# Transposing cached memory keys between query column tiles in a hybrid decoder layer

## The chip, the core and the metric

The kernel runs on one core of one Trainium2 chip. Its time is the device time of one execution in microseconds (us); less is better. TensorE (PE) multiplies and transposes into PSUM; VectorE (DVE), ScalarE (ACT) and GpSimd (POOL) do the rest; SyncE (SP) issues the transfers between DRAM and SBUF.

## What is computed

One inference step of one decoder layer serves two groups with the same weights: a prompt of 512 rows, and eight sampled sequences of four rows each (32 rows). Each sub-layer normalises its input and its output and adds the output to the residual. Everything is float32.

1. A mixer of two head groups (mLSTM and differential attention) with a common input and output projection.
2. Cross-attention, 4 heads of 256, into 256 memory tokens. This is the part that is changed:

```python
def mem_attend(h, mk, mv, w_mq, w_mo):
    q = (h @ w_mq).reshape(B, T, MEM_HEADS, MEM_HEAD_DIM)
    s = jnp.einsum('bqhd,bkhd->bhqk', q, mk) * (MEM_HEAD_DIM ** -0.5)
    p = jax.nn.softmax(s, axis=-1)
    o = jnp.einsum('bhqk,bkhd->bqhd', p, mv).reshape(B, T, D_MODEL)
    return o @ w_mo
```

   The prompt's memory keys and values are projected in the kernel. Those of the eight sequences come from a cache in DRAM (cache_mem_k and cache_mem_v, each 8 x 256 tokens x 1024 columns).
3. A gated feed-forward network with a causal convolution of width 3.

The outputs are both groups' rows, the new keys and values, and the new states.

## The kernel before

All work is written out in Python and recorded instruction by instruction. A scheduler then orders each engine's instructions by a simulated timeline, so the order on an engine is fixed when the program is built, and it need not be that of the source. Tiles come from pools with a fixed number of buffers, in rotation; who takes a buffer waits for the last reader of the tile before it.

**Weights.** A weight tile is loaded into one of six staging buffers (`stage`, tile name wst), and ScalarE and VectorE split it into a high and a low part (`split`, lines 142 and 143) in one of four weight slots (pool `wp`, tag W). The large matmuls multiply high by high, high by low and low by high.

**Queries.** `gemmB` (line 452) makes the query in eight column tiles of 128 columns, 48 matmuls each, over all 544 rows in two halves (256 and 288 rows, alternating). The first four tiles run by halves; the last four, m = 4 to 7, one after the other, each from its own slot. `ev_q` scales a finished tile into qh and ql (prompt) and qs (samples).

**Prompt attention.** `prompt` is a pipeline over 8 steps (head and half of the rows): `ch_soft` makes scores sca (12 matmuls) and the probabilities cp, `ch_turn` transposes them (cpt, 4 transposes) into pT, `ch_out` multiplies by the values (cpo, 12 matmuls for a head). Each `next(prompt)` gives one step of it.

**Sample attention.** Half a sequence's keys, 128 tokens x 1024, is one turn; there are 16. `mk_load` brings it into a staging buffer; `mk_turn` makes eight transposes (tpk, in two PSUM groups of four from a pool of three buffers) and copies them to kT, the first group by ScalarE, the second by VectorE (line 1385). A kT holds a sequence's keys and lies in a weight slot. `mk_scores` makes a sequence's scores: 8 matmuls ssc of 32 columns each, four of which lie beside each other in the array; then the maximum (VectorE) and the exponential (ScalarE). TensorE takes two passes for each of these float32 matmuls, so the trace counts 16 of them where the program has 8. After the eighth sequence `sample_softmax` combines the sums (spa, spt, caz). `mv_load` brings a sequence's values (vt) into a weight slot, and `mv_out` makes 8 matmuls pso with them. The output projection w_mo follows in the same slots.

What sets the order around the change is the loop over `pipe(2 * NB, mk_load, mk_turn, mk_scores)`: it starts behind the last column tile, with prompt steps at `KSTEPS` (3, 7, 11, 15) and the first two value loads at `VLOADS` (13, 15).

Of the kernel before, what the change touches and what calls it, by code (L numbers as in the profile page):

```python
# [18 lines left out]
NB = 8  # L19
# [54 lines left out]
def kernel(ctx: ExitStack, tc: tile.TileContext, I, O):  # L74
# [9 lines left out]
    KSTEPS, VLOADS, NMID, VSTEPS = (3, 7, 11, 15), (13, 15), 3, (0, 1, 3, 5, 6, 7)  # L84
# [13 lines left out]
    def S(shape, dt, name):  # L98
        return sp.tile(list(shape), dt, name=name, tag="S")
# [4 lines left out]
    def T2(shape, name, dt=F32):  # L104
        return t2p.tile(list(shape), dt, name=name, tag="T2")
# [4 lines left out]
    def at(name="at"):  # L110
        return psa.tile([P, 512], F32, name=name, tag="at")

    def mmp(name="mm"):
        return psm.tile([P, 512], F32, name=name, tag="mm")

    def small(w, name, p=P):
        return sm.tile([p, w], F32, name=name, tag=name)
# [5 lines left out]
    def v2(t, b):  # L123
        return t.rearrange("p (a b) -> p a b", b=b)
# [12 lines left out]
    def f32(ap):  # L137
        return ap.bitcast(F32)
# [12 lines left out]
    def con(n, p=P):  # L151
        o, w = CONST_COLS[n]
        return cpk[:p, o:o + w]
# [51 lines left out]
    def stage():  # L205
        return stg.tile([P, 1024], F32, name="wst", tag="st")
# [144 lines left out]
    def pipe(n, *stages):  # L351

        for t in range(n + len(stages) - 1):
            for s in reversed(range(len(stages))):
                if 0 <= t - s < n:
                    stages[s](t - s)
            yield
# [73 lines left out]
    def gemmB(xt, evacs, half_first=False):  # L431

        if half_first:
            slots = [W.get() for _ in evacs]
            for i, (c0, c1) in enumerate(HALF):
                for s, ev in zip(slots, evacs):
                    ps = mmp()[:, :c1 - c0]
                    for k in range(8):
                        for j, (l, x) in enumerate(((0, xt.hi), (0, xt.lo), (1, xt.hi))):
                            mm(ps, lhsT=s[:, l, k, :], rhs=x(k, c0, c1), start=(k == 0 and j == 0), stop=(k == 7 and j == 2))  # L440
                    if i == 1:
                        W.free()
                    ev(i, c0, c1, ps)
                    yield 2.6
            return
        for ev in evacs:
            s = W.get()
            ps = [mmp()[:, :c1 - c0] for c0, c1 in HALF]
            for k in range(8):
                for j, (l, x) in enumerate(((0, xt.hi), (0, xt.lo), (1, xt.hi))):  # L450
                    for i, (c0, c1) in enumerate(HALF):
                        mm(ps[i], lhsT=s[:, l, k, :], rhs=x(k, c0, c1), start=(k == 0 and j == 0), stop=(k == 7 and j == 2))  # L452
                if k % 2 == 1 and k < 7:
                    yield 1.36
            W.free()
            for i, (c0, c1) in enumerate(HALF):
                ev(i, c0, c1, ps[i])
            yield 1.36
# [91 lines left out]
    for i, _ in enumerate(mem_k()):  # L550
        if i in HSTEPS:
            j = HSTEPS.index(i)
# [76 lines left out]
    for c0, c1 in HALF:  # L629
# [5 lines left out]
        t = T2([64, n], "gt")  # L635
# [374 lines left out]
    def sample_exp(sall, b, ps, nm, su):  # L1010
        VRED(out=nm[:, b:b + 1], in_=ps, axis=AX.X, op=MAX, negate=True)
        ACT(out=sall[:, b, :], in_=ps, func=AF.Exp, bias=nm[:, b:b + 1], accum_out=su[:, b:b + 1])
# [294 lines left out]
    def ev_q(m):  # L1307
        if m % 2 == 0:
            qh.append(npool.tile([P, 2, 516], F32R, name="qh", tag="N"))
        if m % 4 == 0:  # L1310
            ql.append(S([P, 4, SEQ], F32R, "ql"))

        def ev(i, c0, c1, ps):
            n = min(c1, SEQ) - c0
            q = qh[m // 2][:, m % 2, c0:c0 + n]
            nc.scalar.mul(out=q, in_=ps[:, :n], mul=1.0 / 16.0)
            STT(out=ql[m // 4][:, m % 4, c0:c0 + n], in0=ps[:, :n], scalar=1.0 / 16.0, in1=f32(q), op0=MUL, op1=SUB)
            if i == 1:
                nc.scalar.mul(out=qs[:, m, :], in_=ps[:, n:n + NS], mul=1.0 / 16.0)
        return ev  # L1320
# [51 lines left out]
    def mk_load(i):  # L1372
        b, c = i // 2, i % 2
        kst[i] = stage()
        dma(out=kst[i], in_=I["cache_mem_k"][0, b, c * P:(c + 1) * P].rearrange("t h d -> t (h d)"))

    def mk_turn(i):
        b, c = i // 2, i % 2
        if c == 0:
            kts[b] = wp.tile([P, 8, 256], F32, name="kT", tag="W")  # L1380
        for q in range(2):
            ps = at("tpk")
            for j in range(4):
                tr(ps[:, j * P:(j + 1) * P], kst[i][:, (4 * q + j) * P:(4 * q + j + 1) * P], ident)  # L1384
            (VCP if q else nc.scalar.copy)(out=kts[b][:, 4 * q:4 * q + 4, c * P:(c + 1) * P], in_=v2(ps, P))

    def mk_scores(i):
        b, c = i // 2, i % 2
        if c == 0:
            return  # L1390
        ps = mmp("ssc")[:, :256]
        for c in range(2):
            for h in range(H):
                mm(ps[NS * h:NS * h + NS], lhsT=qs[:, 2 * h + c], rhs=kts[b][:, 2 * h + c, :], start=(c == 0), stop=(c == 1))  # L1394
        sample_exp(sall, b, ps, nm, su)

    def mv_load(b):
        vts[b] = wp.tile([P, 2, DM], F32, name="vt", tag="W")
        dma(out=vts[b], in_=I["cache_mem_v"][0, b].rearrange("(c p) h d -> p c (h d)", p=P))
# [7 lines left out]
    sall = S([P, NB, 256], F32, "cas")  # L1407
    nm, su = small(NB, "snm"), small(NB, "ssu")
    prompt = pipe(8, ch_soft, lambda i: None, ch_turn, ch_out)
    for i, _ in enumerate(gemmB(hqT, [ev_q(m) for m in range(4, 8)])):  # L1410
        pass
    for t, _ in enumerate(pipe(2 * NB, mk_load, mk_turn, mk_scores)):
        if t in KSTEPS:
            next(prompt, None)
        if t in VLOADS:
            mv_load(VLOADS.index(t))
    _, az = sample_softmax(sall, su, None, con("selX"), "ca")
    for _ in range(NMID):
        next(prompt, None)
# [2 lines left out]
        slotsA(w_mo, n0)  # L1422
    W.nslots = NSLOT
    for b in range(NB):
        if b >= len(VLOADS):
            mv_load(b)
    W.pump()
    for b in range(NB):
# [85 lines left out]
    class Up:  # L1514
# [5 lines left out]
        def ev(self, i, c0, c1, ps):  # L1520
            ti = self.ti
            spread(i)
            if i == 0:
                u = self.u = T2([P, EXT], "u")
                nc.gpsimd.memset(u[:, 0:2], 0.0)
                self.sv = u[:, 2 + SEQ:].rearrange("p (b j) -> p b j", j=6)
                nc.gpsimd.tensor_copy(out=self.sv[:, :, 0:2], in_=v2(cvT[:, ti, 0:16], 2))
                VTT(out=u[:, 2:258], in0=ps, in1=rsb[:, 0:256], op=MUL)  # L1528
                return
            u, sv = self.u, self.sv  # L1530
            VTT(out=u[:, 258:514], in0=ps[:, :256], in1=rsb[:, 256:SEQ], op=MUL)  # L1531
            VTT(out=sv[:, :, 2:6], in0=v2(ps[:, 256:288], TS), in1=v2(rsb[:, SEQ:], TS), op=MUL)
            nc.gpsimd.tensor_copy(out=self.cvo[:, 0:2], in_=u[:, SEQ:SEQ + 2])  # L1533
            nc.gpsimd.tensor_copy(out=v2(self.cvo[:, 2:18], 2), in_=sv[:, :, 4:6])
            c = self.c = T2([P, EXT - 2], "c")
            w = [cvT[:, ti, 16 + j:17 + j] for j in range(3)]
            VTS(out=c, in0=u[:, 2:EXT], scalar1=w[2], scalar2=cvT[:, ti, 19:20], op0=MUL, op1=ADD)
            STT(out=c, in0=u[:, 1:EXT - 1], scalar=w[1], in1=c, op0=MUL, op1=ADD)  # L1538
            STT(out=c, in0=u[:, 0:EXT - 2], scalar=w[0], in1=c, op0=MUL, op1=ADD)  # L1539
# [243 lines left out]
```

## Time and profile before

| | |
|---|---|
| median of 3 runs | 1005.29 us (1005.04 to 1005.99) |
| the profiled execution | 1005.6 us |
| its span | 1003.8 us |
| TensorE busy | 975.0 us, 97% of the span |
| granted TensorE clock, mean | 0.986 |
| last four query column tiles | from about 436 to 460 us |
| transposes and scores of cached keys | 460 to 499 us |
| value sums of the samples | 509 to 532 us |

The profile shows one execution. Times are microseconds from the start of the span, unless marked ns. A row of the order in time has the start, the length from the first instruction's start to the last one's end, engine, line, operation, output and inputs, and count; in brackets stand the idle time ahead and the instruction that ended it. TensorE's matmuls overlap: the next one starts before the last one ends.

### The profile page before, as it was taken

The page shows a single profiled execution, that of the slowest core. Times are in us where ns is not written, and L with a number is a line of the kernel's source. Part 1 is how long each engine was busy: PE and PEld are TensorE (multiplying, and loading weights), DVE is VectorE, ACT ScalarE, POOL GpSimd, SP SyncE. Part 2 cuts the span into 40 slices and gives each one's busy share as a digit, 9 for nine tenths or more (in the row PEclk, how much of TensorE's full clock was granted, in tenths as well). Part 3 has the DMA queues.
Part 4 walks back from the last instruction along what each step waited for, and adds up shares of the span by engine and source line. Part 5 has one row for each costly group of instructions (what it writes and reads, how often), then busy time and mean ns, then how long its engine had stood idle before and what let it go on. Part 6 is the DMA issues. An engine that isn't in the chain of part 4 may idle for free.

```text
span 1003.8 us, 17048 instructions
## 1 busy us (share of the span) xinstructions
PE 975.0 (97%) x6615; PEld 813.2 (81%) x6615; DVE 601.9 (60%) x1129; ACT 388.4 (39%) x746; POOL 195.4 (19%) x389
## 2 busy tenths in 40 slices
PE   8999999999799999999999999999999999999994
PEld 5899777889555778998757789979987997997983
DVE  5735324643686357634653587836857685675677
ACT  5654313334376348633442444242222222222232
POOL 6510000112332124400000264301101010110115
PEclk9999999999799999999999999999999999999998
DMA  8950224152534167764851673052142314214113
GB/s 276 302 156 20 65 84 129 43 182 60 175 115 145 40 210 255 252 206 157 325 199 42 194 236 106 26 146 86 45 116 75 96 46 126 87 44 135 34 47 110
DMA packets 120401, 130.26 MB, mean 130 GB/s; under 512 B 8423, under 2 KB 85832, under 8 KB 120320
## 3 DMA queue, kind: packets, MB, share of 16 engines
q1 hardware_dynamic: 114136, 125.69, 40.6%
q10 hardware_dynamic: 6184, 3.48, 1.2%
q8 instruction: 52, 0.85, 0.3%
q14 instruction: 29, 0.24, 0.1%
HBM read 112.22 MB, written 16.93 MB: 129 GB/s over the span
## 4 chain that ended last, share of the span: by engine, by line
PE 87%; DVE 5%; DMA 4%; issue 2%; ACT 2%; POOL 1%; ACTq 0%; SPq 0%; DVEq 0%; POOLq 0%
PE mm L452 30%; PE mm L440 7%; PE mm L386 6%; PE mm L388 6%; PE mm L387 6%; PE mm L1626 4%; PE mm L1628 4%; PE mm L1627 4%; PE mm L366 3%; PE sda L1179 2%; PE tpk L1384 1%; PE sca L1335 1%; PE cpo L1365 1%; PE ssc L1394 1%; PE oda L1205 1%
## 5 line engine op out<-in xcount | busy, mean ns | idle before, releaser
L142 ACT CAST wslot<-wst 128x1024 fp32r<-128x1024 f32 (+1 forms) x127 | 131.1, 1036 | 278.8 <-issue 81.2
L452 PE MATMUL mm<-fT,wslot 128*128 128x256 f32 (+1 forms) x1872 | 235.7, 288 | 0.0
L452 PEld LDWEIGHTS mm<-fT,wslot 128*128 128x128 f32 x1872 | 234.7, 188 | 0.7 <-issue 0.4
L143 DVE TENSOR_TENSOR wslot<-wst,wslot 128x1024 fp32r<-128x1024 f32 (+1 forms) x127 | 154.0, 1215 | 109.7 <-ACT wslot L142 109.7
L1626 PE MATMUL mm<-wslot,act 128*128 128x512 f32 (+1 forms) x176 | 70.7, 409 | 0.0
L1627 PE MATMUL mm<-wslot,act 128*128 128x512 f32 (+1 forms) x176 | 69.5, 395 | 0.0
L1628 PE MATMUL mm<-wslot,act 128*128 128x512 f32 (+1 forms) x176 | 69.0, 397 | 0.0
L1533 POOL COPY cvo<-u 128x2 f32<-128x2 f32 x43 | 16.1, 375 | 222.8 <-DVE u L1531 222.8
L386 PE MATMUL mm<-wslot,hT 128*128 128x512 f32 x128 | 51.9, 408 | 0.0
L452 PE MATMUL mm<-hT,wslot 128*128 128x288 f32 (+1 forms) x384 | 51.4, 290 | 0.0
L387 PE MATMUL mm<-wslot,hT 128*128 128x512 f32 x128 | 51.2, 400 | 0.0
L388 PE MATMUL mm<-wslot,hT 128*128 128x512 f32 x128 | 50.7, 397 | 0.0
L452 PEld LDWEIGHTS mm<-hT,wslot 128*128 128x128 f32 x384 | 48.9, 188 | 0.9 <-issue 0.8
L1626 PEld LDWEIGHTS mm<-wslot,act 128*128 128x128 f32 (+1 forms) x176 | 33.1, 189 | 17.7 <-issue 8.6
L1528 DVE TENSOR_TENSOR u<-mm,rsb 128x256 f32<-128x256 f32 x43 | 18.1, 423 | 44.2 <-PE mm L452 43.3
L1628 PEld LDWEIGHTS mm<-wslot,act 128*128 128x128 f32 (+1 forms) x176 | 33.0, 188 | 7.5
L1627 PEld LDWEIGHTS mm<-wslot,act 128*128 128x128 f32 (+1 forms) x176 | 33.1, 188 | 6.5
L1545 ACT ACTIVATE c<-c 128x560 f32<-128x560 f32 x21 | 14.1, 672 | 57.3 <-DVE c L1539 57.2
L1539 DVE SCALAR_TENSOR_TENSOR c<-u,cvT,c 128x560 f32<-128x560 f32 x43 | 34.3, 798 | 0.8
L1538 DVE SCALAR_TENSOR_TENSOR c<-u,cvT,c 128x560 f32<-128x560 f32 x43 | 34.1, 794 | 0.1
L1639 DVE TENSOR_TENSOR yp<-mm,yp 128x512 f32<-128x512 f32 x40 | 27.3, 689 | 9.5 <-PE mm L1628 9.4
L386 PEld LDWEIGHTS mm<-wslot,hT 128*128 128x128 f32 x128 | 24.0, 188 | 10.3 <-issue 5.8
(458 smaller groups left out, 1885.8 us busy)
## 6 DMA issues: line engine op xcount, KB each, us to landing
wst<-in_w_up_dram SPq DMA_DIRECT2D x42, 512.0 KB
wst<-in_w_in_dram SPq DMA_DIRECT2D x28, 512.0 KB
wst<-in_w_down_dram SPq DMA_DIRECT2D x20, 512.0 KB
wst<-in_cache_mem_k_dram SPq DMA_DIRECT2D x16, 512.0 KB
vt<-in_cache_mem_v_dram SPq DMA_DIRECT2D x8, 1024.0 KB
wst<-in_w_mk_dram SPq DMA_DIRECT2D x8, 512.0 KB
xb<-in_x_prompt_dram SPq DMA_DIRECT2D x8, 512.0 KB
wst<-in_cache_dk_dram SPq DMA_DIRECT2D x16, 256.0 KB
```

The source lines that it names most:

```text
L142: nc.scalar.copy(out=hi, in_=src)
L143: (eng or nc.vector).tensor_tensor(out=lo, in0=src, in1=f32(hi), op=SUB)
L386: mm(ps[b], lhsT=xt.hi(k, c0, c0 + n), rhs=s[:, 0, kk, :], start=(k == 0), stop=False)
L387: mm(ps[b], lhsT=xt.hi(k, c0, c0 + n), rhs=s[:, 1, kk, :], start=False, stop=False)
L388: mm(ps[b], lhsT=xt.lo(k, c0, c0 + n), rhs=s[:, 0, kk, :], start=False, stop=(k == nk - 1))
L440: mm(ps, lhsT=s[:, l, k, :], rhs=x(k, c0, c1), start=(k == 0 and j == 0), stop=(k == 7 and j == 2))
L452: mm(ps[i], lhsT=s[:, l, k, :], rhs=x(k, c0, c1), start=(k == 0 and j == 0), stop=(k == 7 and j == 2))
L1538: STT(out=c, in0=u[:, 1:EXT - 1], scalar=w[1], in1=c, op0=MUL, op1=ADD)
L1539: STT(out=c, in0=u[:, 0:EXT - 2], scalar=w[0], in1=c, op0=MUL, op1=ADD)
L1626: mm(ps, lhsT=t[:, 0, c0:c0 + P], rhs=s[:n, 0, i % 2, :], start=st, stop=False)
L1627: mm(ps, lhsT=t[:, 0, c0:c0 + P], rhs=s[:n, 1, i % 2, :], start=False, stop=False)
L1628: mm(ps, lhsT=t[:, 1, c0:c0 + P], rhs=s[:n, 0, i % 2, :], start=False, stop=en)
```

## The change

The loop over `pipe` is written out. Six key loads are issued ahead of the last four column tiles. Behind each of these tiles (every fourth step of `gemmB`) stand two turns, one sequence's keys, and the loads of the turns six later; the kT takes the slot that the column tile leaves. Then comes a loop over the sequences: its scores; for the first four, the two turns of the sequence four later; for the last four, a value load. Every second sequence a prompt step follows. So four value loads are issued in this loop instead of two.

```diff
+    for i in range(6):
+        mk_load(i)
     for i, _ in enumerate(gemmB(hqT, [ev_q(m) for m in range(4, 8)])):
-        pass
-    for t, _ in enumerate(pipe(2 * NB, mk_load, mk_turn, mk_scores)):
-        if t in KSTEPS:
+        if i % 4 == 3:
+            for j in (i // 2 - 1, i // 2):
+                mk_turn(j)
+                mk_load(j + 6)
+    for b in range(NB):
+        mk_scores(2 * b + 1)
+        if b < 4:
+            for j in (2 * b + 8, 2 * b + 9):
+                mk_turn(j)
+                if j + 6 < 2 * NB:
+                    mk_load(j + 6)
+        else:
+            mv_load(b - 4)
+        if b % 2 == 1:
             next(prompt, None)
-        if t in VLOADS:
-            mv_load(VLOADS.index(t))
...
-        if b >= len(VLOADS):
+        if b >= 4:
             mv_load(b)
```

What this makes of TensorE's order is seen at three places. The first is the border between the column tiles m = 4 and m = 5 (mm of line 452; hqT is the normalised input, wslot the weight), as a difference:

```order
 L452 MATMUL mm<-hqT_4081,wslot 128x256
 L452 MATMUL mm<-hqT_4081,wslot 128x288
+L1384 MATMUL tpk<-cpk,wst 128x128 x12
 L452 MATMUL mm<-hqT_4069,wslot 128x256
 L452 MATMUL mm<-hqT_4069,wslot 128x288
```

Twelve transposes now stand here, and the last four of the two turns 18 matmuls later, inside the next tile. The same pair of 12 and 4 stands behind m = 5 and m = 6.

The second place is among the transposes and scores (ssc) that follow the columns. Before, TensorE has there:

```order
L1394 MATMUL ssc<-kT,qs 32x256 x6
L1384 MATMUL tpk<-cpk,wst 128x128 x16
L1394 MATMUL ssc<-kT,qs 32x256 x8
L1384 MATMUL tpk<-cpk,wst 128x128 x12
L1394 MATMUL ssc<-kT,qs 32x256 x2
L1384 MATMUL tpk<-cpk,wst 128x128 x4
```

And now, directly behind the last column tile:

```order
L1384 MATMUL tpk<-cpk,wst 128x128 x12
L1394 MATMUL ssc<-kT,qs 32x256 x14
L1384 MATMUL tpk<-cpk,wst 128x128 x4
L1394 MATMUL ssc<-kT,qs 32x256 x2
L1384 MATMUL tpk<-cpk,wst 128x128 x8
```

No run of transposes is longer than 12, and scores of two sequences stand in one run of 14. The runs of scores are now 14, 2, 5, 3, 8, 8, 2, 6, 2, 6, 2, 6; before they were 2, 6, 8, 2, 6, 8, 2, 6, 2, 6, 2, 6, 2, 6. The runs of value sums (pso) are now 12, 9, 4, 1, 3, 3, 16, 8, 8; before 6, 10, 6, 4, 2, 3, 2, 15, 8, 8.

The third place is the end of the sample softmax (spa and spt) and the prompt's fifth transposes (cpt). Before:

```order
L1365 MATMUL cpo<-pT,mvN 128x512 x8
L1031 MATMUL spa<-cas,csz 32x256 x8
L1365 MATMUL cpo<-pT,mvN 128x512 x4
L1036 MATMUL spt<-cpk,spc 128x128 x2
L1353 MATMUL cpt<-cpk,cp 128x128
```

Now spa stands ahead of a whole step of prompt scores, of which this is the beginning:

```order
L1335 MATMUL sca<-mkT,ql 128x256
L1353 MATMUL cpt<-cpk,cp 128x128 x4
L1031 MATMUL spa<-cas,csz 32x256 x8
L1335 MATMUL sca<-mkT,qh 128x256 x2
L1335 MATMUL sca<-mkT,ql 128x256
```

And behind these twelve sca follow the same products and the fifth transposes:

```order
L1335 MATMUL sca<-mkT,ql 128x256
L1365 MATMUL cpo<-pT,mvN 128x512 x8
L1036 MATMUL spt<-cpk,spc 128x128 x2
L1365 MATMUL cpo<-pT,mvN 128x512 x4
L1353 MATMUL cpt<-cpk,cp 128x128
```

So 12 sca and 12 cpo lie between spa and the fifth cpt, where 4 cpo lay before. On SP, ten key loads are issued ahead of the small loads for the convolution (cr), where six were; and four loads of w_mo ahead of the first value load, where two were.

## The prediction

> **What bounds the kernel now.** I read the page first, then a table of stretches around the edit, then TensorE's instructions in order of time in those stretches.
>
> ```profile
> span 1003.8 us, 17048 instructions
> PE 975.0 (97%) x6615; PEld 813.2 (81%) x6615; DVE 601.9 (60%) x1129; ACT 388.4 (39%) x746; POOL 195.4 (19%) x389
> PE 87%; DVE 5%; DMA 4%; issue 2%; ACT 2%; POOL 1%; ACTq 0%; SPq 0%; DVEq 0%; POOLq 0%
> ```
>
> TensorE is busy for 97% of the span, and 87% of the chain that ended last is TensorE. The table (stretch, its length, then busy time of each engine, granted clock, DMA share, GB/s) holds the four last query columns, the keys and scores, the value sums, and the memory output projection.
>
> ```profile
> 436.00:460.20 24.20, 24.20 (x197) 24.20 (x196) 3.83 (x8) 4.33 (x14) 1.81 (x1) 1.00 0.24 83
> 460.20:504.40 44.20, 43.22 (x369) 31.78 (x371) 27.10 (x57) 21.00 (x61) 0.00 (x0) 1.00 0.83 291
> 504.40:534.00 29.60, 28.85 (x236) 18.02 (x235) 15.36 (x32) 14.91 (x44) 0.00 (x0) 1.00 0.40 144
> 534.00:560.00 26.00, 26.00 (x162) 18.84 (x161) 12.11 (x26) 9.71 (x21) 0.00 (x0) 1.00 0.26 76
> ```
>
> TensorE is full in all four at clock 1.00. So the columns have no idle time into which the transposes could go: the change can only pay by making TensorE's steps shorter or by removing its waits. The rows of TensorE (start, time from the first start to the last end, line, operation, count; in brackets the idle time ahead, and who ended it):
>
> ```profile
> 436.13 24.11 PE L452 MATMUL mm<-hqT,wslot 128*128 128x256 f32 x192
> 460.08 2.55 PE L1384 MATMUL tpk<-cpk,wst 128*128 128x128 f32 x20
> 462.56 0.62 PE L1394 MATMUL ssc<-kT,qs 128*32 128x256 f32 x4
> ...
> 467.98 0.66 PE L1384 MATMUL tpk<-cpk,wst 128*128 128x128 f32 x4 [0.35 <-DVE kT L1385]
> 468.57 1.07 PE L1394 MATMUL ssc<-kT,qs 128*32 128x256 f32 x16
> 469.57 1.53 PE L1384 MATMUL tpk<-cpk,wst 128*128 128x128 f32 x12
> 471.03 0.63 PE L1394 MATMUL ssc<-kT,qs 128*32 128x256 f32 x4
> 471.58 0.66 PE L1384 MATMUL tpk<-cpk,wst 128*128 128x128 f32 x4
> 472.00 0.48 PE L1335 MATMUL sca<-mkT,qh 128*128 128x256 f32 x2
> ...
> 473.58 1.06 PE L1394 MATMUL ssc<-kT,qs 128*32 128x256 f32 x12
> 474.57 1.53 PE L1384 MATMUL tpk<-cpk,wst 128*128 128x128 f32 x12
> 476.45 0.66 PE L1384 MATMUL tpk<-cpk,wst 128*128 128x128 f32 x4 [0.35 <-DVE kT L1385]
> ...
> 494.00 0.63 PE L1394 MATMUL ssc<-kT,qs 128*32 128x256 f32 x4 [0.29 <-ACT kT L1385]
> 494.56 3.06 PE L1365 MATMUL cpo<-pT,mvN 128*128 128x512 f32 x12
> ...
> 504.29 1.07 PE L1031 MATMUL spa<-cas,csz 128*32 128x256 f32 x16
> 505.29 1.19 PE L1365 MATMUL cpo<-pT,mvN 128*128 128x512 f32 x4
> ...
> 507.45 0.30 PE L1353 MATMUL cpt<-cpk,cp 128*128 128x128 f32 x1 [0.75 <-DVE cp L1344]
> ...
> 511.01 1.49 PE L1404 MATMUL pso<-vt,caz 128*32 128x256 f32 x20
> 512.43 0.50 PE L1335 MATMUL sca<-mkT,qh 128*128 128x256 f32 x2
> ...
> 521.88 1.93 PE L1404 MATMUL pso<-vt,caz 128*32 128x256 f32 x30
> 523.74 1.66 PE L1365 MATMUL cpo<-pT,mvN 128*128 128x512 f32 x6
> ```
>
> To be seen here: only four waits of note (0.35, 0.35, 0.29, 0.75), and that a run's price is not its count. Matmuls overlap, so a run's price is the distance to the next start: 16 of the scores (a whole sequence, each counted twice here, in two passes) take 1.00 us (468.57 to 469.57), 12 take 0.99 (473.58 to 474.57), 4 still take 0.55 (471.03 to 471.58). A sequence cut into 4 and 12 so costs 1.54 instead of 1.00.
>
> **What moves, and its price, term by term.** All 128 transposes, 64 scores, 64 value sums and the prompt's work remain; TensorE's order alone changes, between 442 and 538 us. In the new order, 48 transposes (turns 0 to 5) stand in six runs of 12 and 4 behind column tiles; the rest and all scores stand behind the last column. Past the first tiles of the output projection the order is the same as before, so what is gained by there is kept, as long as TensorE stays the bound: the row of 534.00 to 560.00 is full.
>
> *Transposes.* Between scores, 12 take 1.46 us (469.57 to 471.03), 0.122 each; the first 20 up to 462.56 are no cheaper. Between matmuls of the columns' kind there is a row elsewhere:
>
> ```profile
> 592.48 4.99 PE L440 MATMUL mm<-fT,wslot 128*128 128x256 f32 x40
> 597.30 1.03 PE L317 MATMUL tp<-cpk,xb 128*128 128x128 f32 x8
> 598.09 2.86 PE L440 MATMUL mm<-fT,wslot 128*128 128x256 f32 x22
> ```
>
> Eight take 0.79 us there, 0.099 each, and the columns' own step (4.82 us for 40) doesn't suffer. 48 x (0.122 - 0.099) = 1.1 us; the columns' stretch grows by 4.8 us and the later one shrinks by 5.9. I take 1.0.
>
> *Scores and value sums.* From the runs above (counts halved to instructions): 2 to 4 instructions 0.55, 5 to 8 1.00, 9 to 12 1.42 (511.01 to 512.43), 13 to 16 1.86 (521.88 to 523.74). Score runs before: six of 2, six of 6, two of 8, 11.2 us. After: 14, 2, 5, 3, 8, 8, and three times 2 and 6: 10.6. Value sums before: 6, 10, 6, 4, 2, 3, 2, 15, 8, 8: 9.5; after: 12, 9, 4, 1, 3, 3, 16, 8, 8: 8.9. Together 1.2 us less.
>
> *Waits that go.* The two of 0.35 are the fourth group of four transposes in a run of 16: three PSUM buffers hold three groups, and the fourth waits for a copy. No run is longer than 12 now. The 0.29 is a score right behind its last transposes; now six scores (1.00 us) stand between, and the copy takes 0.59:
>
> ```profile
> L1384 PE MATMUL tpk<-cpk,wst x128: 272/273/332, 460.1 to 493.4; 128*128 128x128 f32 x128
> L1385 ACT COPY kT<-tpk x16: 575/587/601, 460.8 to 493.4; 128x512 f32<-128x512 f32 x16
> L1385 DVE COPY kT<-tpk x16: 682/692/692, 461.2 to 493.8; 128x512 f32<-128x512 f32 x16
> ```
>
> The 0.75 is a prompt transpose 3.16 us behind the start of spa (504.29 to 507.45): ScalarE's exponentials queue behind the copy of spa. Now twelve sca and twelve cpo and two small transposes stand between, by the rows above 1.5 + 3.0 + 0.2 us on top of spa's 1.0: nearly 6 us where 3.2 are needed. The brackets sum to 1.74 us; with the restart of a stopped pipeline (467.98 follows a run whose twelve steps ended near 467.4) 2.3. I take 2.0.
>
> *What could wait newly.* Six of the sixteen turns' copies come into the columns: 6 x 0.587 = 3.5 us on ScalarE and 6 x 0.692 = 4.2 on VectorE, which have 4.33 and 3.83 of 24.20 us busy there. They queue between the evacuations of a column, and TensorE waits for them only by a PSUM buffer: the run of 4 stands 18 column matmuls (18 x 0.125 = 2.2 us) behind the run of 12. The scale copy qs queues behind one key copy; who waits is the eighth score, behind 12 transposes. I take nothing; the bound is one wait like that of 467.98 at each of the six places, 6 x 0.57 = 3.4 us. Below nothing it can't go, since a wait removed is counted above.
>
> *Queues.* SP's rows of the cached keys:
>
> ```profile
> 427.49 11.55 SPq L1375 DMA_DIRECT2D wst<-in_cache_mem_k_dram  x6
> 461.15 0.35 SPq L1375 DMA_DIRECT2D wst<-in_cache_mem_k_dram  x1
> ```
>
> The seventh load waits today until a transpose frees a staging buffer. Now four of them go out by 455 us, while DMA is at 0.24, and the queue after 460 (0.83) is lightened; no TensorE row above waits for a load, so I put this at nothing. The small convolution loads are passed by these four; their consumer is TensorE's work at 538. A key tile takes the slot that a finished column left, so no weight is late. GpSimd's order is unchanged.
>
> *Sum.* -1.0 - 1.2 - 2.0 = -4.2 us: the span of 1003.8 becomes 999.6. The profiled execution took 1005.6, 1.8 more than its span, and so would take 1001.4; the median of the runs, 1005.29, lies 0.3 below it: **1001.1 us**.
>
> **A rule weighed against a row.** The clock after the projection:
>
> ```profile
> 586.79:590.20 3.41, 3.41 (x18) 3.41 (x18) 3.41 (x6) 1.66 (x3) 1.41 (x4) 0.50 0.94 260
> ```
>
> For 3.41 us the clock was 0.50, right after TensorE's short idle time at 582 to 586; that costs up to 1.7 us. The stretch lies behind the edit and moves by some 4 us. If the gap falls otherwise into the clock's windows, the 1.7 us can go, or come twice. I keep 1.7 on either side for the range. The Trainium skill (TensorE: Matmul & The Clock Gate, Part 1) says that these windows of about 3.4 us run freely and don't start with the kernel; by that rule the place is chance, and my centre stays.
>
> **The rivals.**
> *Waits come back elsewhere.* The scheduler's order doesn't know the real waits; copies could stop TensorE as often as before. Then only -1.0 - 1.2 remain: 1003.1 us. For it: ScalarE's queue in the columns is longer; against it: the distances above, each at least 1 us longer than the copy. 0.20.
> *Given back behind the edit.* The last four value loads start when the first value sums free a slot. One of these pairs is closer together now, 8 us by the run prices instead of 10. If it, or the projection's weights behind it, were late by 3 us or more, the time would be about 1004.9. Against it: no value sum waits for DMA today, with DMA at 0.40. 0.08.
> *Slower: transposes don't step, they occupy.* If a transpose among column matmuls held TensorE for its whole 0.273 us (the row of durations above), 48 x (0.273 - 0.099) = 8.4 us would be added: 1009.5. It decides from 0.19 us a transpose on, where 48 x 0.087 eat the 4.2. Against it: eight in 0.79 us among such matmuls at 597.30. 0.07. The Trainium skill's same page, Part 4, gives about 275 ns for such a transpose in a kernel and says that it does not count as busy for the clock; the duration agrees with 273, but the step is 0.11, and the clock was 1.00 through 32 us that were half transposes.
> That the change doesn't do what it says is ruled out by the order: six runs do stand among the columns.
>
> **How the numbers follow.** Forecast 0.65, waits back 0.20, given back 0.08, slower 0.07. A change below 0.2% (2.0 us) can't be told from none here, so faster means below 1003.3. The forecast's own range is 999.4 (clock stretch gone) to 1002.8 (a second one, or half of the new waits' bound). To leave out no more than 2 in 10 it goes up past 1003.1 to 1004.0; the slower end and the given-back case stay out. Faster: 0.65 and about half of the second case, 0.76. Same: the other half and the third, 0.17. Slower: 0.07.
>
> **What would show it.** Right: six tpk runs among the rows of L452, with no bracket and steps of about 0.10; the columns' stretch 4.8 us longer; spa some 6 to 7 us earlier; the work of cvp (now at 538) at about 534; no bracket at cpt. Wrong: brackets at tpk or ssc that name kT; the last columns longer by 8 us or more; an idle TensorE between the value sums and the projection that names vt or wslot; a stretch at clock 0.50 that is new.

## The result and the profile after

The changed kernel takes 1000.97 us (median of 8 runs, 1000.05 to 1003.89); the kernel before took 1005.16 us beside it (8 runs, 1004.16 to 1008.64). The ratio is 0.9961 [0.9947, 0.9975]: 0.4% faster, 4.2 us. The forecast was 1001.1 us. The profiled execution took 1001.39 us.

The page of the changed kernel:

```profile
span 999.6 us, 17060 instructions
PE 970.7 (97%) x6615; PEld 811.2 (81%) x6615; DVE 599.6 (60%) x1129; ACT 389.3 (39%) x746; POOL 196.1 (20%) x389
PE 84%; DMA 5%; DVE 5%; issue 2%; POOL 1%; ACT 1%; SPq 0%; DVEq 0%; POOLq 0%; ACTq 0%
```

TensorE still bounds it. Its work is the same 6615 matmuls; its busy time fell with the span. The stretches of the same work (columns, keys and scores, value sums, output projection):

```profile
436.00:465.30 29.30, 29.30 (x242) 29.30 (x241) 7.83 (x15) 7.54 (x19) 1.81 (x1) 1.00 0.57 174
465.30:498.50 33.20, 33.20 (x297) 24.00 (x296) 19.65 (x46) 17.16 (x52) 0.00 (x0) 1.00 0.74 245
498.50:530.00 31.50, 31.50 (x260) 20.94 (x259) 17.75 (x38) 16.21 (x47) 0.00 (x0) 1.00 0.50 187
530.00:556.00 26.00, 26.00 (x161) 18.85 (x160) 12.14 (x25) 9.37 (x21) 0.00 (x0) 1.00 0.24 74
```

TensorE is busy for the whole length of all four; before, the second and the third had 0.98 and 0.75 us idle. The copies of six turns now lie in the columns: VectorE's 3.83 us there became 7.83, ScalarE's 4.33 became 7.54. TensorE in order of time:

```profile
436.33 6.15 PE L452 MATMUL mm<-hqT,wslot 128*128 128x256 f32 x48
442.32 1.47 PE L1384 MATMUL tpk<-cpk,wst 128*128 128x128 f32 x12
443.55 2.51 PE L452 MATMUL mm<-hqT,wslot 128*128 128x256 f32 x18
445.89 0.60 PE L1384 MATMUL tpk<-cpk,wst 128*128 128x128 f32 x4
446.25 4.00 PE L452 MATMUL mm<-hqT,wslot 128*128 128x256 f32 x30
450.08 1.47 PE L1384 MATMUL tpk<-cpk,wst 128*128 128x128 f32 x12
...
465.60 1.47 PE L1384 MATMUL tpk<-cpk,wst 128*128 128x128 f32 x12
467.00 1.93 PE L1394 MATMUL ssc<-kT,qs 128*32 128x256 f32 x28
468.86 0.66 PE L1384 MATMUL tpk<-cpk,wst 128*128 128x128 f32 x4
469.45 1.05 PE L1394 MATMUL ssc<-kT,qs 128*32 128x256 f32 x4
470.43 1.09 PE L1384 MATMUL tpk<-cpk,wst 128*128 128x128 f32 x8
...
499.00 1.07 PE L1031 MATMUL spa<-cas,csz 128*32 128x256 f32 x16
504.55 0.27 PE L1353 MATMUL cpt<-cpk,cp 128*128 128x128 f32 x1
506.49 1.50 PE L1404 MATMUL pso<-vt,caz 128*32 128x256 f32 x24
```

No row here has a bracket. To compare kernels without the differences elsewhere in the program I use one distance: from the first matmul of the last four columns (line 452) to the last matmul of the output projection (line 388). Both stand in the groups by line (durations in ns, then first and last start). Before:

```profile
L452 PE MATMUL mm<-hqT,wslot x192: 276/286/298, 436.1 to 459.9; 128*128 128x256 f32 x96, 128*128 128x288 f32 x96
L388 PE MATMUL mm<-wslot,oT x64: 387/396/475, 527.4 to 582.0; 128*128 128x512 f32 x64
```

And after:

```profile
L452 PE MATMUL mm<-hqT,wslot x192: 276/288/366, 436.3 to 465.5; 128*128 128x256 f32 x96, 128*128 128x288 f32 x96
L388 PE MATMUL mm<-wslot,oT x64: 387/396/475, 523.7 to 578.4; 128*128 128x512 f32 x64
```

From 436.1 to 582.0 are 145.9 us, from 436.3 to 578.4 are 142.1: the edit itself is worth 3.8 us. The columns, first to last matmul, grew from 23.8 to 29.2.

### The profile page after: what moved, and what is told of

Read it like the earlier page. It is cut to its first block, busy times and chain, and to the rows that moved or that the text cites. A ratio compares the mean times of both kernels' runs of the same rounds, so it can differ in the third digit from the quotient of the medians.

```text
span 999.6 us, 17060 instructions
## 1 busy us (share of the span) xinstructions
PE 970.7 (97%) x6615; PEld 811.2 (81%) x6615; DVE 599.6 (60%) x1129; ACT 389.3 (39%) x746; POOL 196.1 (20%) x389
## 4 chain that ended last, share of the span: by engine, by line
PE 84%; DMA 5%; DVE 5%; issue 2%; POOL 1%; ACT 1%; SPq 0%; DVEq 0%; POOLq 0%; ACTq 0%
PE mm L452 31%; PE mm L386 6%; PE mm L387 6%; PE mm L388 6%; PE mm L440 5%; PE mm L1638 4%; PE mm L1640 4%; PE mm L1639 4%; PE mm L366 3%; PE sda L1179 2%; PE tpk L1384 2%; PE cpo L1365 1%; PE sca L1335 1%; PE ssc L1394 1%; PE oda L1205 1%
## 5 line engine op out<-in xcount | busy, mean ns | idle before, releaser
L452 PE MATMUL mm<-fT,wslot 128*128 128x256 f32 (+1 forms) x1872 | 235.7, 288 | 0.0
L452 PEld LDWEIGHTS mm<-fT,wslot 128*128 128x128 f32 x1872 | 234.7, 188 | 0.7 <-issue 0.4
L452 PE MATMUL mm<-hT,wslot 128*128 128x288 f32 (+1 forms) x384 | 51.4, 290 | 0.0
L388 PE MATMUL mm<-wslot,hT 128*128 128x512 f32 x128 | 50.7, 397 | 0.0
L452 PEld LDWEIGHTS mm<-hT,wslot 128*128 128x128 f32 x384 | 48.9, 188 | 0.9 <-issue 0.8
```

Source lines behind the costliest of these rows:

```text
L388: mm(ps[b], lhsT=xt.lo(k, c0, c0 + n), rhs=s[:, 0, kk, :], start=False, stop=(k == nk - 1))
```

## The experiments

Single executions of one kernel differ by several us (in one of the comparisons below, 29 runs of the kernel before took 1003.35 to 1010.36). So the table gives the ratio of the times as it was recorded, with its 95% interval (the quotient of the medians can differ from it: for the doubled transposes it is 1.0034), and, for sizes, the two distances of the profiled execution, read as above. Each kernel was profiled once; the columns' part repeats (23.8 in the four kernels without transposes in it, 29.1 or 29.2 in the four with 48). The kernel before took 1005.98 us beside the first four experiments and 1006.41 beside the last three.

| kernel | median us | ratio to before | columns (L452) | L452 to last L388 | against before |
|---|---|---|---|---|---|
| before | | | 436.1 to 459.9: 23.8 | to 582.0: 145.9 | |
| after | 1000.97 | 0.9961 [0.9947, 0.9975] | 436.3 to 465.5: 29.2 | to 578.4: 142.1 | -3.8 |
| prompt steps later | 1004.49 | 0.9980 [0.9965, 0.9995] | 433.8 to 457.6: 23.8 | to 577.9: 144.1 | -1.8 |
| after, prompt steps earlier | 1002.65 | 0.9973 [0.9958, 0.9989] | 433.8 to 462.9: 29.1 | to 577.8: 144.0 | -1.9 |
| before, whole scores | 1001.88 | 0.9955 [0.9940, 0.9970] | 436.4 to 460.2: 23.8 | to 577.8: 141.4 | -4.5 |
| after, second pool | 998.96 | 0.9931 [0.9907, 0.9955] | 435.4 to 464.5: 29.1 | to 574.3: 138.9 | -7.0 |
| before, whole scores and second pool | 1006.76 | 1.0019 [0.9999, 1.0038] | 435.4 to 459.2: 23.8 | to 583.6: 148.2 | +2.3 |
| after, late loads | 1004.07 | 0.9982 [0.9963, 1.0000] | 434.8 to 463.9: 29.1 | to 579.0: 144.2 | -1.7 |
| after, doubled transposes | 1009.79 | 1.0057 [1.0040, 1.0075] | 434.7 to 469.1: 34.4 | to 584.5: 149.8 | +3.9 |

**Prompt steps later, without any transpose between the columns.** The kernel before, with each of the prompt's four steps two ticks of the loop later:

```diff
-    KSTEPS, ... = (3, 7, 11, 15), ...
+    KSTEPS, ... = (5, 9, 13, 17), ...
```

> The kernel before, with its four prompt steps two ticks later (KSTEPS 5, 9, 13, 17), as in the changed kernel; all transposes stay behind the columns. This gives the changed kernel's value-sum runs (12, 9, 4, 1, 3, 3, 16, 8, 8) and its place of spa, but runs of 16 transposes stay. My theory (the gain is made of TensorE's waits and runs, and only part of it has to do with the columns): value sums -0.6 us, other switches -0.2, the wait at the fifth prompt transposes gone (-0.9); the waits in runs of 16 stay: -1.7 us against before, about 1003.5. Rival (the gain comes from what stands between the columns and from key loads that start earlier): no change, 1005.2.

Measured: 1.8 us less in the distance. The waits that are left, in TensorE's order of time:

```profile
469.25 0.66 PE L1384 MATMUL tpk<-cpk,wst 128*128 128x128 f32 x4 [0.35 <-DVE kT L1385]
477.71 0.66 PE L1384 MATMUL tpk<-cpk,wst 128*128 128x128 f32 x4 [0.35 <-DVE kT L1385]
489.72 0.63 PE L1394 MATMUL ssc<-kT,qs 128*32 128x256 f32 x4 [0.24 <-ACT kT L1385]
```

The 0.75 at cpt has gone with no transpose moved. It and the value sums' better runs are a product of the prompt's new places, not of the columns. The two waits of 0.35 stay, and of the one at the last scores 0.24 is left.

**The other way round.** The changed kernel, with the prompt's steps behind every sequence of even number, so that they come one sequence earlier:

```diff
-        if b % 2 == 1:
+        if b % 2 == 0:
             next(prompt, None)
```

> The changed kernel, with its four prompt steps after the scores of sequences 0, 2, 4 and 6 instead of 1, 3, 5 and 7; the transposes stay between the columns and the key loads stay early. Score runs become 7, 1, 12, 1, 3, 2, 3, 11, 6, 1, 1, 2, 6, 2, 6 and value sums 6, 5, 6, 4, 2, 6, 3, 16, 8, 8. My theory: by the run prices 2.4 us of the 4.2 us are lost, 1003.4 (no new wait at the fifth prompt transposes, since 11 cpo stand ahead of them). Rival (the columns and the early loads make the gain): it stays, 1001.0.

Measured: 1.9 us of the 3.8 are given back (by the distance; the intervals of the two kernels' times overlap). No wait over 0.2 us came back between the columns and the projection; the loss lies in worse runs of scores and value sums. Both edits put about half of the gain on the places of the prompt's steps.

**Whole scores.** The kernel before, with the four heads of a sequence's scores in another order, the heads of VectorE's copy first, so that all eight scores wait for the last copy and stay together:

```diff
-            for h in range(H):
+            for h in (2, 3, 0, 1):
```

> The kernel before, with the heads of a score in the order 2, 3, 0, 1, so that no score run starts before all its keys are copied: all score runs are of 8, and transposes stand in runs of 24, 16, 16, 16, 16, 16, 16 and 8. By the run prices 4.1 us less. My theory on the waits (the fourth group of four transposes in a run waits for a copy, 0.57 us each): three in the run of 24 and one in each of six runs of 16, 5.1 us, against 1.3 us of such waits before; together about -0.3 us, 1004.9. Rival (long runs of transposes don't wait, the two waits seen were chance): -4 us, 1001.

My forecast of 0.3 us less fell, and the rival, 4 us less, came true: 4.5 us less, more than the change under study, from one line. TensorE's order of time shows why:

```profile
460.38 2.98 PE L1384 MATMUL tpk<-cpk,wst 128*128 128x128 f32 x24
463.29 1.07 PE L1394 MATMUL ssc<-kT,qs 128*32 128x256 f32 x16
465.83 1.94 PE L1384 MATMUL tpk<-cpk,wst 128*128 128x128 f32 x16
467.69 1.07 PE L1394 MATMUL ssc<-kT,qs 128*32 128x256 f32 x16
...
490.44 1.07 PE L1394 MATMUL ssc<-kT,qs 128*32 128x256 f32 x16 [0.84 <-DVE kT L1385]
```

Each sequence's scores are one run of 16 passes for 1.00 us, and runs of 16 and 24 transposes have no bracket: 465.83 to 467.69 is 1.86, where the run at 466.10 of before took 2.47 to its scores. From start to start all scores take 8.01 us, where before took 11.27. No transpose waits for a key load either. VectorE in this kernel:

```profile
466.91 0.69 DVE L1385 COPY kT<-tpk 128x512 f32<-128x512 f32 x1 [0.18 <-PE tpk L1384]
467.80 0.69 DVE L1385 COPY kT<-tpk 128x512 f32<-128x512 f32 x1 [0.20 <-PE tpk L1384]
```

And in the kernel before, at the same place:

```profile
467.24 0.69 DVE L1385 COPY kT<-tpk 128x512 f32<-128x512 f32 x1 [0.59 <-PE tpk L1384]
```

This copy begins 1.14 us behind its run's first transpose (466.10) in before and ends at 467.93, just ahead of the fourth group at 467.98. With whole scores it begins 1.08 us behind it (465.83) and ends at 467.60, when the fourth group is nearly through. So the copies were not faster; there the fourth group began at 467.14, ahead of this copy's end, and so did not wait for it. Which buffer it took, the trace doesn't say.

**The version that beats both.** The changed kernel, with the second group of each turn in the other PSUM pool, that of the columns and scores:

```diff
-            ps = at("tpk")
+            ps = mmp("tpk") if q else at("tpk")
```

> The changed kernel, with every second group of four transposes in the matmuls' PSUM pool (five buffers) instead of the pool of three. The transposes of a sequence then stand whole, 16 behind each column, and scores in runs of 7, 1, 8, 8, 8, 16, 16. By the run prices 2.5 us less than the changed kernel: 998.5. Rival (the pool of five, now shared with the columns, the prompt scores and the sums, makes them wait): 1001 or more.

Measured: 998.96 us, 0.7% below before; the distance is 7.0 us shorter, 3.2 more than the change alone brings. TensorE's order of time:

```profile
441.37 1.91 PE L1384 MATMUL tpk<-cpk,wst 128*128 128x128 f32 x16
443.04 6.27 PE L452 MATMUL mm<-hqT,wslot 128*128 128x256 f32 x48
...
475.43 1.97 PE L1384 MATMUL tpk<-cpk,wst 128*128 128x128 f32 x16
477.33 1.07 PE L1394 MATMUL ssc<-kT,qs 128*32 128x256 f32 x16
```

Both turns of a sequence stand in one run of 16 without a bracket, and nearly all scores in whole runs.

**Whole scores and second pool, without the columns.** The kernel before, with the two one-line edits just shown (head order and second pool). The head order keeps the scores whole here, as they nearly are in the version above:

> The kernel before, transposes behind the columns and key loads late as there, with the heads of a score in the order 2, 3, 0, 1 and every second group of transposes in the matmuls' PSUM pool. All score runs are whole (8 times 8), as in nearly all of the second-pool kernel, but nothing stands between the columns. My theory (the place between the columns is worth little by itself; whole runs and no waits are what pays): by the run prices 4.1 us less than before and 0.7 more than the second-pool kernel; with one wait of some 0.8 us at the last scores, about 3 to 4 us faster than before, and not over 2 us behind the second-pool kernel. Rival (the columns carry most of the gain): within 1 us of before.

This expectation fell. The time can't be told from that of before (1.0019 [0.9999, 1.0038]); the distance is 2.3 us longer than before, 6.8 longer than with whole scores alone, and 9.3 longer than the second pool gave with the columns. TensorE's order of time has new waits (four of eight rows with a wait over 0.5 us):

```profile
471.14 0.63 PE L1384 MATMUL tpk<-cpk,wst 128*128 128x128 f32 x4 [1.35 <-DMA wst<-in_cache_mem_k_dram]
...
477.38 0.63 PE L1384 MATMUL tpk<-cpk,wst 128*128 128x128 f32 x4 [1.00 <-DMA wst<-in_cache_mem_k_dram]
478.89 0.63 PE L1384 MATMUL tpk<-cpk,wst 128*128 128x128 f32 x4 [0.88 <-DMA wst<-in_cache_mem_k_dram]
...
487.32 0.66 PE L1384 MATMUL tpk<-cpk,wst 128*128 128x128 f32 x4 [0.88 <-DMA wst<-in_cache_mem_k_dram]
```

With a fifth row of this kind (0.52 at 475.73) these are 4.6 us of waiting for key loads; three waits of scores (0.51, 0.51 and 1.37) come to 2.4 more. SyncE's rows of the loads:

```profile
468.94 4.77 SPq L1375 DMA_DIRECT2D wst<-in_cache_mem_k_dram  x3
475.24 0.33 SPq L1375 DMA_DIRECT2D wst<-in_cache_mem_k_dram  x1
481.17 1.61 SPq L1375 DMA_DIRECT2D wst<-in_cache_mem_k_dram  x2
```

And the last such row with whole scores alone:

```profile
474.21 3.25 SPq L1375 DMA_DIRECT2D wst<-in_cache_mem_k_dram  x3
```

There, too, all transposes stand behind the columns and a load begins only when a transpose has freed a staging buffer. Yet no transpose waits for a load: the last load has gone out 17.1 us behind the first transpose (460.38 to 477.46), here 23.4 behind it (459.36 to 482.78). So the place behind the columns does not make the loads late by itself; they came late in the order that the second pool gave. One cause is seen: in this kernel's queue on SyncE a value load, which waits for a slot, stands ahead of the last two key loads (481.17). But that can explain only the last of the five waits, since the other four end by 478.89; why those loads were late is open.

**Late loads.** The changed kernel with its transposes between the columns, but with the seventh and later loads held back until the last column's scale copy (small additions on GpSimd touch the staging buffers and read qs). In the source, two turns move behind the columns for that; on TensorE they stood there already.

> The changed kernel with six turns between the columns, but the key loads from the seventh on wait for the last column's query, as they waited in the kernel before (a tiny GpSimd sum of the staging buffer and the last query is added to make them wait, its result unused). TensorE's order is nearly that of the changed kernel (0.8 us more by the run prices). My theory: early loads add nothing by themselves but are needed here, since the next turns come right behind the columns: one wait of 2 to 5 us of a transpose for its load, so 3 to 6 us lost against the changed kernel, about 1005. Rival (the loads' place does not matter): 0.8 us lost, 1002.

In between: 2.1 us lost against after, where I had said 3 to 6 and the rival 0.8. Two waits for loads came:

```profile
470.21 1.06 PE L1384 MATMUL tpk<-cpk,wst 128*128 128x128 f32 x8 [0.61 <-DMA wst<-in_cache_mem_k_dram]
471.50 1.22 PE L1384 MATMUL tpk<-cpk,wst 128*128 128x128 f32 x8 [0.22 <-DMA wst<-in_cache_mem_k_dram]
```

They are 0.83 of the 2.1; by the run prices of the expectation 0.8 are worse runs; the rest, some 0.5, is open.

**Doubled transposes.** The changed kernel with each of the 64 transposes of turns 0 to 7 made twice into the same place:

```diff
-            for j in range(4):
+            for j in [k for k in range(4) for _ in range(times)]:
...
-                mk_turn(j)
+                mk_turn(j, 2)
```

> The changed kernel, with each of the 64 transposes of the first eight turns made twice into the same place, so that the columns' stretch holds 48 more (24 and 8 where 12 and 4 stood) and 16 more follow it. My theory (a transpose between column matmuls costs its step): 0.11 us each, the columns' stretch longer by 5.2 us and the whole by 7 to 8 us, about 1008.5. Rival (it occupies TensorE for its 0.27 us): the columns' stretch longer by 13 us, the whole by 17.

Between the first and the last column matmul stand 48 transposes more, and this distance grew from 29.2 to 34.4 us: 0.108 us each. At 0.273 each it would have grown by 13. The whole distance grew by 7.7, within the 7 to 8 expected; the median lies 1.3 us above the 1008.5 expected.

## Why the prediction was right, and where not

Each TensorE start in the trace, with the time to the next start given to its kind, makes a ledger from the first column to the first cvp, work for the convolution that stands among the projection's matmuls (538.08 before, 534.42 after; us):

| kind | before | after | difference |
|---|---|---|---|
| column matmuls | 23.95 | 24.53 | +0.58 |
| transposes tpk, with the waits behind them | 16.90 | 14.29 | -2.61 |
| spt, with the wait at cpt | 1.13 | 0.14 | -0.99 |
| scores ssc | 11.27 | 11.02 | -0.25 |
| value sums pso | 9.50 | 8.96 | -0.54 |
| prompt: sca, cpt, cpo | 28.84 | 28.80 | -0.04 |
| sum | | | -3.85 |

The kinds left out (spa, the projection's matmuls, ost) differ by 0.01 or less.

**Waits that go (forecast -2.0): right, -2.3.** From start to start they cost 0.51, 0.51, 0.36 and 0.92, which is what the brackets plus the restart were estimated at. All four are gone and none came in their place. But the reason given for the two of 0.35 was half right: "No run is longer than 12 now" is not what removed them. Whole scores runs 16 and 24 transposes through the same three buffers without a wait, and the run of 20 at 460.08 in before had none either. What fits all of these is that it counts whose buffer the next group takes and when that copy ends; as the trace doesn't name the buffers, this is argued, not shown. At cpt the reason held, though spa came 5.3 us earlier (504.29 to 499.00), not 6 to 7.

**Transposes (forecast -1.0): mis-sized, about -0.65** (the -2.61 without the 1.38 of the first three waits, and the +0.58 of the columns). The run itself goes as the quoted row said: 12 in 1.23 us (442.32 to 443.55). Overlooked was the way back: the first column matmul starts 0.03 us behind the last transpose, where a transpose's own step is 0.109, but the second one 0.205 behind the first, where 0.125 is usual. The 0.08 that the last step seems to save is paid one step later, in each of six runs. In the quoted row of eight this return lies among the 22 matmuls behind it, and the prediction had looked at the 40 ahead. The columns' stretch grew by 5.3 us (465.60 - 436.33 against 460.08 - 436.13), 0.111 a transpose, not 4.8.

**Scores and value sums (forecast -1.2): mis-sized, -0.8.** The value sums came as priced (-0.54 for -0.6). The scores gave 0.25 instead of 0.65. In the rows of after, the run of 4 passes at 469.45 takes 0.98 us to the next start, not the 0.55 of its price. That is 0.43, the whole miss. The single starts in the traces show why. Passes that start within 0.03 us of each other form a group, and a run costs by its groups, not by its passes: in the runs of scores and value sums without a wait, two groups take 0.55 to 0.57 us, four 0.98 to 1.00, six 1.41 to 1.43 and eight 1.84 to 1.87, whether a group has four passes or one. The run of 4 that gave the price (471.03 in before) is two groups of two; this one is four groups of one, 0.21 to 0.24 apart. It is what the run of 28 ahead of it left over, which has four groups of four and four of three. So the unit of the price table, the number of matmuls, was wrong, and for most runs it made no difference.

**Early loads at nothing: right for this edit.** Nothing waited for a key load before or after. SyncE's rows of after show ten loads issued by 455 us, where before had six, and the eleventh behind them:

```profile
427.87 26.74 SPq L1375 DMA_DIRECT2D wst<-in_cache_mem_k_dram  x10
458.91 0.35 SPq L1375 DMA_DIRECT2D wst<-in_cache_mem_k_dram  x1
```

What the early loads are worth beyond that is only partly shown. Held back, they cost 2.1 us, 0.83 of it in waits for loads, and one order without the columns lost 4.6 us waiting for loads. But whole scores alone, without the columns and with its loads as late as in before, waits for no load and is 0.7 us shorter than the change (141.4 against 142.1). So a gain of this size doesn't need the place between the columns, and the loads bind only in some orders. With the scores whole, or nearly so, on both sides, the columns, the early loads and the second pool together are worth 2.5 us (138.9 against 141.4). The 9.3 us between 138.9 and 148.2 are not the columns' worth, since the second pool without the columns made waits that whole scores alone doesn't have. Two kernels that would separate this were not run: the changed one with whole scores and the pool of three, and the one before with the second pool alone.

**New waits at nothing: right.** Copies of six turns did queue in the columns without a bracket on TensorE.

**The clock: the span agrees by luck.** The projection ends 3.8 us earlier (by the sum, 4.2), and the span is shorter by 4.2. So it is partly luck that the forecast of 1001.1 came within 0.2 of the measured 1000.97. The difference was made behind the projection, by two things that cancel in part. TensorE behind the idle gap after the projection, before and after (same 19 matmuls):

```profile
586.27 4.03 PE L440 MATMUL mm<-fT,wslot 128*128 128x256 f32 x19 [0.28 <-POOL fT L143]
```

```profile
582.42 2.50 PE L440 MATMUL mm<-fT,wslot 128*128 128x256 f32 x19 [0.28 <-POOL fT L143]
```

The stretch at clock 0.50 is absent in the execution after, as its table of stretches shows:

```profile
580.40:583.80 3.40, 2.63 (x17) 2.03 (x17) 3.40 (x4) 2.02 (x5) 2.15 (x3) 1.00 0.74 200
583.80:587.20 3.40, 3.40 (x32) 3.40 (x31) 3.40 (x6) 1.52 (x3) 2.21 (x3) 1.00 1.05 288
587.20:590.60 3.40, 3.40 (x31) 3.40 (x30) 1.73 (x6) 0.62 (x1) 2.89 (x8) 1.00 1.06 330
```

That gave 1.5 us. About 1.1 were lost again 15 us later, around a wait for GpSimd that before does not have at this place:

```profile
597.42 2.79 PE L440 MATMUL mm<-fT,wslot 128*128 128x288 f32 x19 [0.57 <-POOL fT L143]
```

The bound of 1.7 either way held. The columns don't decide whether the stretch is there: of the nine profiled executions six have one 3 to 5 us behind the projection's last matmul, among them three with transposes between the columns (second pool, late loads, doubled transposes); three have none (after, and both shifts of the prompt's steps). With prompt steps later, the profiled execution took 1000.92 where the kernel's median is 1004.49. That the stretch comes and goes between executions of one kernel is likely but not shown, since each kernel was profiled once. It would agree with the Trainium skill (TensorE: Matmul & The Clock Gate, Part 1), which has the windows of some 3.4 us run freely.

**The rivals.** Waits elsewhere: none. Given back behind the edit: the 3.8 us stand at the end of the projection. Slower, because a transpose occupies TensorE: refuted by the doubled transposes, 0.108 us against the 0.19 from which it would decide. (The 275 ns that the prediction takes from the Trainium skill, TensorE: Matmul & The Clock Gate, Part 4, stand there for bf16; the float32 transposes here lasted 273.)

## What to carry to other kernels

Price a run of overlapping matmuls by the distance to the next start, its way in and its way back included, and for side-by-side tiles by the groups that start together: keeping the groups whole was worth as much here as moving the whole phase. When work is moved ahead, ask which loads its end sets free: holding them back cost 2.1 us here, though no wait for a load had been seen. A run's length alone doesn't say whether it will wait; look for the copy that the waiting instruction needs and for its end.

## What the runs showed that was not expected

Side-by-side scores of 32 columns cost by the group of passes that start together: two groups 0.55 us, four 1.00, six 1.42, eight 1.86. So a sequence in one run (16 passes, four groups) takes 1.00 us, and cut into 4 and 12 passes it takes 1.54, since those make six groups. The first matmul behind a run of transposes comes early (0.03 us) and the second late (0.205), so a price read up to the first one is 0.08 us too low. A change of one line in the order of four heads moved the projection's end by 4.5 us.
